# A feed-forward down product computed as seven half products over quadrants

## Chip, cores and metric

The kernel runs on one core of one Trainium2 chip. The metric is the device time of one execution in microseconds (us), as the median of several runs; lower is better. TensorE (PE in the profile) multiplies, VectorE (DVE) and ScalarE (ACT) work on elements, SyncE (SP) issues all the transfers.

## The reference, cut to what matters

Two batches of tokens (512 and 256, together T = 768) pass through two layers with the same weights. Each layer has a norm, two mixers, an output product with a residual, a second norm and a feed-forward block; a last norm ends the trunk.

```python
x = x + jnp.einsum('bsd,de->bse', merged, w_out)
h = rmsnorm(x, norm_ffn_g)
hid = jnp.square(jax.nn.relu(jnp.einsum('bsd,df->bsf', h, w_ff1)))     # 1024 -> 4096
return x + jnp.einsum('bsf,fd->bsd', hid, w_ff2)                       # 4096 -> 1024
```

## The kernel before, in words

Activations mostly lie with features in partitions, as tiles of 128 features by 768 tokens. Each fp32 operand of a dense product is split into a part rounded to fp32r ("hi") and the rest ("lo"), and a product is three passes: hi·hi, hi·lo and lo·hi. `wunit` (L148) loads 512 KB of weights in one transfer, rounds them on ScalarE (L156) and subtracts on VectorE (`sub`, L106, called in L157). `side[0]` is VectorE from the first layer's mixers on.

All dense products stand in one stream of items. An item's body runs matrix groups through `mm_group` (L215), and the next item's weights are made ahead by one item (`make_units`). `feat_dense` gives features in partitions and goes through the tokens in two ranges, `SPLITS`: 512 and 256. `tok_dense` gives tokens in partitions: six blocks of 128 tokens, 256 output columns wide. Accumulators of these groups come from the pool `pac`, three PSUM banks; five other banks are in the pool `pmx` (`pm`).

The program is recorded through a framework that schedules it: on each engine the instructions stand in the order that its scheduler chose, which is near the written one but interleaves neighbours, and each engine then goes through its own list in order.

The feed-forward block (L1047 to L1087) goes through the 4096 inner features in four chunks of 1024. Up: eight tiles of 128 features, each with 24 matmuls per token range; L1061 applies relu and the norm's factor on VectorE, L1062 squares on ScalarE, L1063 and L106 make hi and lo of the hidden tile. Down in the first layer: eight column tiles of `w_ff2`, each 24 matmuls per token range, and `evac2` adds the accumulator to the residual `xT` (L1070); in the last chunk it also feeds the next layer's norm (`Norm.add`: L288, L289, L297, L298) and stores `xT` (`spill`, L849). Down in the second layer: `tok_dense` in four slices of 256 columns, after `Last.to_tokens` has turned the residual around by 48 transposes (L796); `Last.add` adds (L802) and, in the last chunk, norms and stores each block of tokens as it is done.

```python
            nc.vector.tensor_tensor(x, x, acc[:, :n], op=ALU.add)                    # L1070, before
            out = Last(xT)                                                           # L1081
```

After the first layer's block the second layer begins with the values of its softmax mixer (`tok_dense`, L892, 256 or 288 columns wide): their evacuation (L877, L878) needs the tokens' 1/rms, which comes out of ones-matmuls over the norm's sums (L334), and small steps on ScalarE and VectorE (L337, L354 to L359).

## Time and profile before

| | |
|---|---|
| time, median of 3 runs | 3077.69 us (3076.8 to 3079.48) |
| profiled execution: span from first to last instruction | 3075.7 us |
| TensorE matmuls busy | 3051.5 us, 99% of the span |
| VectorE busy | 1574.4 us, 51% |
| ScalarE busy | 1229.8 us, 40% |
| granted TensorE clock, mean | 0.998 of full speed |

The page gives the span of the profiled execution; a time of its own is not listed beside the three runs, which lie 1.1 to 3.8 us above the span. "Busy" counts an engine's instructions with their overlap taken out. TensorE's busy share is near the whole, so what counts in most stages is how many matmul columns there are, and where another engine or a transfer makes TensorE wait.

### The profile page before, as it was taken

Reading aid. Unit: us, or ns where it says so; the run is one execution under the profiler, and the core shown is the slowest. Engines: PE = TensorE matmul, PEld = TensorE weight load, DVE = VectorE, ACT = ScalarE, POOL = GpSimd, SP = SyncE. Lnnn points to the kernel's source line nnn. Section 1 sums busy time; section 2 is a strip of 40 time slices with the busy share of each in tenths; the row PEclk is TensorE's granted clock in tenths of the full one; section 3 lists DMA queues with packets and bytes.
Section 4 is the critical chain, followed back from the end, with each engine's and each line's share of the span. In section 5 each row is a group of like instructions: output and inputs, shape, how many; then the busy total and the mean of one; then the engine's idle time right before and its main releaser. Section 6 shows DMA issues by size and latency. Waiting matters only on the chain.

```text
span 3075.7 us, 49458 instructions
## 1 busy us (share of the span) xinstructions
PE 3051.5 (99%) x20048; PEld 2763.5 (90%) x20048; DVE 1574.4 (51%) x3419; ACT 1229.8 (40%) x2709; POOL 7.5 (0%) x7
## 2 busy tenths in 40 slices
PE   8999999999999999999999999999999999999998
PEld 7988889999888888888899888899988889999998
DVE  5456667665445423333553666677744553333334
ACT  4555565544223313222343655655532233222133
POOL 0000000000000000000000000000000000000000
PEclk9999999999999999999999999999999999999999
DMA  6533322222422222222354233332233322222222
GB/s 210 186 80 84 90 77 82 67 73 72 134 93 78 62 68 63 62 62 65 98 166 137 73 84 89 83 94 69 59 112 98 103 62 62 62 62 62 63 69 69
DMA packets 371892, 268.05 MB, mean 87 GB/s; under 512 B 37552, under 2 KB 345040, under 8 KB 371664
## 3 DMA queue, kind: packets, MB, share of 16 engines
q1 hardware_dynamic: 371664, 264.89, 29.4%
q8 instruction: 158, 2.59, 0.4%
q14 instruction: 70, 0.57, 0.1%
HBM read 217.50 MB, written 47.33 MB: 86 GB/s over the span
## 4 chain that ended last, share of the span: by engine, by line
PE 95%; DMA 2%; DVE 2%; ACT 1%; SPq 0%; issue 0%; POOL 0%; ACTq 0%; DVEq 0%
PE acc L215 86%; PE op L524 2%; PE go L735 1%; PE pt L510 1%; PE sp L487 1%; PE up L713 1%; PE cp L657 1%; PE ap L695 1%; DMA l_dram<-b 0%; DMA v<-v_dram 0%; PE sp L483 0%; DMA raw<-in_w_in 0%; PE tp L764 0%; PE sp L481 0%; PE kp L684 0%
## 5 line engine op out<-in xcount | busy, mean ns | idle before, releaser
L215 PE MATMUL acc<-hh,whi 128*128 128x256 f32 (+1 forms) x2560 | 884.8, 346 | 0.3 <-DVE rl L1061 0.3
L215 PE MATMUL acc<-hl,whi 128*128 128x256 f32 (+1 forms) x2560 | 863.0, 337 | 0.0
L215 PE MATMUL acc<-hh,wlo 128*128 128x256 f32 (+1 forms) x2560 | 861.7, 337 | 0.0
L156 ACT CAST whi<-raw 128x1024 fp32r<-128x1024 f32 x320 | 335.7, 1049 | 602.7 <-PE acc L215 564.8
L215 PEld LDWEIGHTS acc<-hh,whi 128*128 128x128 f32 x2560 | 485.5, 190 | 55.5 <-DVE rl L1061 0.5
L215 PEld LDWEIGHTS acc<-hh,wlo 128*128 128x128 f32 x2560 | 484.8, 189 | 52.7
L215 PEld LDWEIGHTS acc<-hl,whi 128*128 128x128 f32 x2560 | 486.1, 190 | 41.6 <-issue 0.5
L106 DVE TENSOR_TENSOR wlo<-raw,whi 128x1024 fp32r<-128x1024 f32 (+1 forms) x317 | 388.3, 1225 | 155.0 <-ACT whi L156 152.4
L215 PE MATMUL acc<-whi,hh 128*128 128x256 f32 (+1 forms) x1344 | 390.1, 291 | 2.7 <-DVE vst L878 1.4
L215 PE MATMUL acc<-whi,hl 128*128 128x256 f32 (+1 forms) x1344 | 383.0, 285 | 3.0 <-DVE hl L289 2.8
L215 PE MATMUL acc<-wlo,hh 128*128 128x256 f32 (+1 forms) x1344 | 382.9, 285 | 0.8 <-POOL wlo L106 0.8
L215 PEld LDWEIGHTS acc<-whi,hl 128*128 128x128 f32 x1344 | 258.4, 192 | 5.1 <-DVE hl L289 3.6
L215 PEld LDWEIGHTS acc<-whi,hh 128*128 128x128 f32 x1344 | 258.3, 192 | 5.0 <-issue 2.6
L215 PEld LDWEIGHTS acc<-wlo,hh 128*128 128x128 f32 x1344 | 257.9, 192 | 1.1 <-POOL wlo L106 1.1
L215 PE MATMUL acc<-whi,hih 128*128 128x256 f32 x768 | 217.3, 283 | 0.0
L215 PE MATMUL acc<-whi,hil 128*128 128x256 f32 x768 | 217.3, 283 | 0.0
L215 PE MATMUL acc<-wlo,hih 128*128 128x256 f32 x768 | 217.3, 283 | 0.0
L1062 ACT ACTIVATE rl<-rl 128x512 f32<-128x512 f32 (+1 forms) x128 | 66.9, 523 | 274.5 <-DVE rl L1061 274.5
L215 PE MATMUL acc<-hil,whi 128*128 128x256 f32 (+1 forms) x512 | 172.4, 337 | 0.0
L215 PE MATMUL acc<-hih,whi 128*128 128x256 f32 (+1 forms) x512 | 172.3, 336 | 0.0
L215 PE MATMUL acc<-hih,wlo 128*128 128x256 f32 (+1 forms) x512 | 172.0, 336 | 0.0
L1061 DVE SCALAR_TENSOR_TENSOR rl<-acc,nr 128x512 f32<-128x512 f32 (+1 forms) x128 | 71.4, 558 | 181.9 <-PE acc L215 174.5
(232 smaller groups left out, 4785.3 us busy)
## 6 DMA issues: line engine op xcount, KB each, us to landing
raw<-in_w_in SPq DMA_DIRECT2D x152, 512.0 KB, 4.0
raw<-in_w_ff SPq DMA_DIRECT2D x128, 512.0 KB, 4.2
v_dram<-vst SPq DMA_DIRECT2D x72, 256.0 KB, 2.3
v<-v_dram SPq DMA_DIRECT2D x64, 128.0 KB, 4.7
raw<-in_w_branch_b SPq DMA_DIRECT2D x16, 512.0 KB, 4.3
raw<-in_w_out SPq DMA_DIRECT2D x16, 512.0 KB, 4.4
x_dram<-xT SPq DMA_DIRECT2D x16, 384.0 KB, 2.3
la_dram<-le SPq DMA_DIRECT2D x24, 256.0 KB, 3.4
```

The source lines that it names most:

```text
L106: eng.tensor_tensor(out, x, hi.bitcast(F32), op=ALU.subtract)
L156: nc.scalar.copy(hi, raw)
L215: nc.tensor.matmul(acc[:, :n], wt, xt, start=(k == 0 and j == 0), stop=(k == nkt - 1 and j == 2))
L487: nc.tensor.matmul(sp[hh][:, (g - 1) * 128:g * 128], q[g][pb, bs], k[g][pb, bs], start=True, stop=True)
L510: nc.tensor.transpose(pt[0:kx[g], g, hh, :], pr[hh][:, c0[g]:c0[g] + kx[g]], ident)
L524: nc.tensor.matmul(op[:, hh], v[ks, hh].rearrange("p s c -> p (s c)"), pT[g][ks, hh].rearrange("p s c -> p (s c)"), start=(g == 0), stop=( ...
L657: nc.tensor.matmul(cp[:, j, :], x[:, j, dc], cumT[:, d, :], start=(i == 0), stop=(i == 1))
L695: nc.tensor.matmul(ap[-1][:, j, :], ek[:, j, :], eq[:, j, :], start=True, stop=True)
L713: nc.tensor.matmul(up, x, y, start=(i == 0), stop=(i == 2))
L735: nc.tensor.matmul(op, x, y, start=(i == 0), stop=(i == len(mm) - 1))
L1061: nc.vector.scalar_tensor_tensor(r, acc[:, :n], 0.0, fnorm.r[:, t0:t0 + n], op0=ALU.max, op1=ALU.mult)
L1062: nc.scalar.activation(r, r, AF.Square)
```

## The change

The down product of the feed-forward block is written as Strassen's scheme in Winograd's form. The inner features come in eight chunks of 512; the tokens in two halves of 384 (`HALVES`), in the up product and the output product too. For each chunk, `quad_dense` has four items m = 0..3; item m computes the output feature tiles m and m + 4 for both halves of the tokens, from a 2 by 2 arrangement of weights (A11 to A22, each 256 by 128) and of hidden tiles (B11 to B22, each 256 by 384). Seven products take the place of eight. Each product is six matmuls of 384 columns (two inner tiles by three passes). Their operands are sums: S1 to S4 of weights (`wquad`, four VectorE operations, then hi and lo of each) and T1 to T4 of hidden tiles (`Quads.second`). The sums of products are made in PSUM: bank A takes A11·B11, S2·T2, S3·T3 and A22·T4 one after the other, and after each the running sum is added to one quadrant of `xT` on VectorE; bank C takes S1·T1 and S4·B22 in this way, bank B takes A12·B21. The banks come from `pmx`. The last two products of an item are kept in `later` and run between groups of what follows. In the last chunk the additions feed `Norm.add` (first layer) or the new `Last.add` (second layer).

Both layers now use this form, with features in partitions. In the second layer the result is turned around at the end: `Last.to_tokens` makes 12 transposes per m, those of the last m after all products, then the norm's factor, and 12 stores. The constants of the mixers (`dist`, `cumT`, `mask`, and the buffers `glT`, `wgate`) move from a pool that lasts into one that is opened at each layer's mixers, so they are loaded once more in the second layer.

```diff
+HT = T // 2
+HALVES = ((0, HT), (HT, HT))
...
+    def mixer_constants(pool):
+        dist = pool.tile([128, 3, 256], F32, name="dist")
+        cumT = pool.tile([128, 2, 256], F32R, name="cumT")
+        mask = pool.tile([128, 256], U8, name="mask")
         nc.sync.dma_start(out=dist, in_=a["alibi"])
...
+        scope.update(dist=dist, cumT=cumT, mask=mask,
+                     glT=pool.tile([98, T], F32R, name="glT"),
+                     wgate=pool.tile([98, 1024], F32R, name="wgate"))
...
+                if not stream and later:
+                    current.append(one_later())
...
+    later = deque()
+
+    def one_later():
+        if later:
+            yield from later.popleft()()
...
-                    for t0, n in SPLITS:
+                    for t0, n in splits:
                         yield from feat_tile(units[0], ci, x, t0, n, i + ci, evac)
+                        yield from one_later()
...
+    def split2(x, hi, lo):
+        nc.scalar.copy(hi, x)
+        sub(lo, x, hi)
+        return hi, lo
...
+        def first(self, p, x):
+            if self.b11 is None:
+                self.b11 = b3("b11h", F32R, (128, 2, HT)), b3("b11l", F32R, (128, 2, HT))
+            self.x[p] = x
+            self.ops["B11", p] = split2(x[:, 0:HT], *(y[:, p] for y in self.b11))
...
+        def second(self, p, y):
+            x = self.x[p]
+            b11, b12, b21, b22 = x[:, 0:HT], x[:, HT:T], y[:, 0:HT], y[:, HT:T]
+            t13, t24 = b3("t13"), b3("t24")
+            t1, t3, t2, t4 = t13[:, 0:HT], t13[:, HT:T], t24[:, 0:HT], t24[:, HT:T]
+            nc.vector.tensor_tensor(t1, b12, b11, op=ALU.subtract)
+            nc.vector.tensor_tensor(t3, b22, b12, op=ALU.subtract)
+            nc.vector.tensor_tensor(t2, b22, t1, op=ALU.subtract)
+            nc.vector.tensor_tensor(t4, b21, t2, op=ALU.subtract)
+            for z, names in ((y, ("B21", "B22")), (t13, ("T1", "T3")), (t24, ("T2", "T4"))):
+                hi, lo = split2(z, b3("qh", F32R), b3("ql", F32R))
+                for i, name in enumerate(names):
+                    self.ops[name, p] = hi[:, i * HT:(i + 1) * HT], lo[:, i * HT:(i + 1) * HT]
...
+    def wquad(w, m):
...
+        src = [w[:, (m + 4 * i) * 128:(m + 4 * i + 1) * 128].rearrange("(k p) c -> p k c", p=128) for i in range(2)]
+        nc.sync.dma_start(out=raw[:, 0:4], in_=src[0])
+        nc.sync.dma_start(out=raw[:, 4:6], in_=src[1][:, 2:4])
+        nc.sync.dma_start(out=raw[:, 6:8], in_=src[1][:, 0:2])
+        a11, a12, a22, a21 = (raw[:, 2 * i:2 * i + 2] for i in range(4))
+        s12, s43 = (b3(n, shape=(128, 4, 128)) for n in ("s12", "s43"))
+        s1, s2, s4, s3 = s12[:, 0:2], s12[:, 2:4], s43[:, 0:2], s43[:, 2:4]
+        ah, al = (wsp.tile([128, 6, 128], F32R, tag="w", name=n) for n in ("ah", "al"))
+        nc.vector.tensor_tensor(s1, a21, a22, op=ALU.add)
+        nc.vector.tensor_tensor(s2, s1, a11, op=ALU.subtract)
+        split2(raw[:, 0:6], ah, al)
+        nc.vector.tensor_tensor(s4, a12, s2, op=ALU.subtract)
+        nc.vector.tensor_tensor(s3, a11, a21, op=ALU.subtract)
+        ops = {n: (ah[:, 2 * i:2 * i + 2], al[:, 2 * i:2 * i + 2]) for i, n in enumerate(("A11", "A12", "A22"))}
+        for s, names in ((s12, ("S1", "S2")), (s43, ("S4", "S3"))):
+            hi, lo = split2(s, *(scope["ws"].tile([128, 4, 128], F32R, tag="ws", name=n) for n in ("sh", "sl")))
+            for i, n in enumerate(names):
+                ops[n] = hi[:, 2 * i:2 * i + 2], lo[:, 2 * i:2 * i + 2]
+        return ops
+
...
+                def product(an, bn, bank, dests):
+                    def g():
+                        if bank not in banks:
+                            banks[bank] = pm("w" + bank), True
+                        acc, new = banks[bank]
+                        banks[bank] = acc, False
+                        ah, al = units[0][an]
+                        for p in range(quads.n):
+                            bh, bl = quads.ops[bn, p]
+                            for j, (x, y) in enumerate(passes(ah[:, p], al[:, p], bh, bl)):
...
+                                nc.tensor.matmul(acc[:, :HT], x, y, start=(new and p == 0 and j == 0),
+                                                 stop=(p == quads.n - 1 and j == 2), skip_group_check=True)
+                        for i, k in dests:
+                            add_to(m + 4 * i, k, acc[:, :HT])
+                        yield quads.n * 3 * HT / 2400
+                    return g
+
+                yield from product("A11", "B11", "A", [(0, 0)])()
+                yield from one_later()
+                yield from product("S1", "T1", "C", [(1, 1)])()
+                yield from product("A12", "B21", "B", [(0, 0)])()
+                yield from one_later()
+                yield from product("S2", "T2", "A", [(0, 1)])()
+                yield from product("S4", "B22", "C", [(0, 1)])()
+                later.append(product("S3", "T3", "A", [(1, 1)]))
+                later.append(product("A22", "T4", "A", [(1, 0)]))
+            return f
+
+        for m in range(4):
+            add([lambda m=m: wquad(w, m)], body(m))
...
+            if t0 not in self.acc:
+                self.acc[t0] = b3("lacc", shape=(128, n))
+                nc.scalar.activation(self.acc[t0], x, AF.Square)
+            else:
+                sq = b3("lsq", shape=(128, n))
+                nc.scalar.activation(sq, x, AF.Square)
+                nc.vector.tensor_tensor(self.acc[t0], self.acc[t0], sq, op=ALU.add)
+            nc.scalar.activation(x, x, AF.Copy, scale=gfin[:, k:k + 1])
+            m = k % 4
+            self.left[m] -= 1
+            if self.left[m] == 0:
+                self.to_tokens(m)
...
+        def to_tokens(self, m):
+            last = len(self.y) == NT and not any(self.left)
+            if last:
+                r = self.rms()
+            for b in range(NT):
+                if b not in self.y:
+                    self.y[b] = b3("ya", shape=(128, 2, 384))
+                y = self.y[b]
+                tp = pm("tp", (128, 2, 128))
                 for i in range(2):
...
+                rb = r[:, b:b + 1]
+                z = b3("yb", shape=(128, 2, 128))
+                nc.scalar.activation(z, tp, AF.Copy, scale=rb)
+                nc.vector.tensor_scalar(y, y, rb, None, op0=ALU.mult)
+                out, row = (y_prompt, b) if b < 4 else (y_sample, b - 4)
+                out = out.rearrange("o s d -> (o s) d")[row * 128:(row + 1) * 128].rearrange("t (i c) -> t i c", i=2)
+                nc.sync.dma_start(out=out[:, :, 0:384], in_=y)
+                nc.sync.dma_start(out=out[:, :, 384:512], in_=z)
...
+        mixer_constants(mixers.enter_context(tc.tile_pool(name=f"mxc{l}", bufs=1)))
...
+        scope["ws"] = ffn.enter_context(tc.tile_pool(name=f"wsq{l}", bufs=7))
...
-        feat_dense(a["w_out"][l], 0, mg, evac, ncol=DM)
+        feat_dense(a["w_out"][l], 0, mg, evac, ncol=DM, splits=HALVES)
...
-        for c in range(4):
...
-                    nc.scalar.copy(hh, r)
-                    sub(hl, r, hh)
...
-            def evac2(k, t0, n, acc, xT=xT, c=c, norm=norm):
-                x = xT[k][:, t0:t0 + n]
-                nc.vector.tensor_tensor(x, x, acc[:, :n], op=ALU.add)
...
-            if not last:
-                feat_dense(w2, 0, hid, evac2, ncol=DM)
-                continue
-            if c == 0:
-                out = Last(xT)
-                weave([lambda b=b, i=i: out.to_tokens(b, i) for b in range(NT) for i in range(2)], 40)
-            for u in range(4):
-                tok_dense(lambda v, u=u, w2=w2: [(w2[v * 512:(v + 1) * 512, u * 256:(u + 1) * 256], 256)], 256, hid,
-                          lambda b, acc, u=u, c=c: out.add(b, acc, u, c))
...
+                r = f3("rl", shape=(128, n))
+                nc.vector.scalar_tensor_tensor(r, acc[:, :n], 0.0, fnorm.r[:, t0:t0 + n], op0=ALU.max, op1=ALU.mult)
+                nc.scalar.activation(q[0][:, t0:t0 + n], r, AF.Square)
+                if i < 2 and t0 == 0:
+                    chunks[c].first(i, q[0])
+                elif i >= 2 and t0:
+                    chunks[c].second(i - 2, q[0])
+
...
+            def add_to(k, half, acc):
+                t0 = half * HT
+                x = xT[k][:, t0:t0 + HT]
+                nc.vector.tensor_tensor(x, x, acc, op=ALU.add)
+                left[k, half] = left.get((k, half), 1 if k >= 4 and half == 0 else 2) - 1
+                if c < 7 or left[k, half]:
+                    return
+                if last:
+                    out.add(k, x, t0, HT)
+                    return
+                norm.add(k, x, t0, HT)
+                if left.get((k, 1 - half), 1) == 0:
+                    spill(k)
+
+            quad_dense(a["w_ff2"][l][c * 512:(c + 1) * 512, :], chunks[c], add_to)
+
+        for c in range(8):
+            tiles = [4 * c + i for i in (0, 2, 1, 3)]
+            for i, t in enumerate(tiles):
+                up(t)
+                if i == (3 if c == 7 else 0) and c:
+                    down(c - 1)
```

On TensorE, in the first layer's down product, the rows before are those of one accumulator that takes 24 matmuls in a row (`hih`, `hil` are hi and lo of a hidden tile, `whi`, `wlo` of the weights); the first of them are:

```order
L215 MATMUL acc_11745<-hih_11203,whi_11673 128x512
L215 MATMUL acc_11745<-hil_11204,whi_11673 128x512
L215 MATMUL acc_11745<-hih_11203,wlo_11674 128x512
L215 MATMUL acc_11745<-hih_11294,whi_11673 128x512
L215 MATMUL acc_11745<-hil_11295,whi_11673 128x512
```

Now, in a chunk of the first layer (wA_12193, wB_12209 and wC_12201 are the banks of item 0, wA_12253 is bank A of item 1; `qh`, `ql`, `b11h` are hi and lo of the hidden operands, `ah`, `sh`, `sl` of the weights):

```order
L341 MATMUL wB_12209<-qh_12076,al_12095 128x384
L341 MATMUL wA_12253<-b11h_11549,ah_12177 128x384
L341 MATMUL wA_12193<-qh_11931,sh_12102 128x384
L341 MATMUL wA_12193<-ql_11932,sh_12102 128x384
L341 MATMUL wA_12193<-qh_11931,sl_12103 128x384
L341 MATMUL wA_12193<-qh_12084,sh_12102 128x384
L341 MATMUL wA_12193<-ql_12085,sh_12102 128x384
L341 MATMUL wA_12193<-qh_12084,sl_12103 128x384
L341 MATMUL wC_12201<-qh_11923,sh_12106 128x384
L341 MATMUL wC_12201<-ql_11924,sh_12106 128x384
L341 MATMUL wC_12201<-qh_11923,sl_12107 128x384
```

A bank is taken up again after one or two products into other banks, and one matmul of the next item stands ahead of S2·T2.

On VectorE at the same places, before:

```order
L1070 TENSOR_TENSOR xT_10592<-xT_10592,acc_11745 128x512
L1070 TENSOR_TENSOR xT_10592<-xT_10592,acc_11771 128x256
L106 TENSOR_TENSOR wlo_11858<-raw_11855,whi_11857 128x1024
L1070 TENSOR_TENSOR xT_10594<-xT_10594,acc_11803 128x512
L1070 TENSOR_TENSOR xT_10594<-xT_10594,acc_11829 128x256
```

and now, in the middle of a chunk's four items (s12, s43 are sums of weights, sl and al their lo parts):

```order
L108 TENSOR_TENSOR sl_12246<-s12_12235,sh_12245 128x512
L1197 TENSOR_TENSOR xT_10603<-xT_10603,wA_12253 128x384
L1197 TENSOR_TENSOR xT_10609<-xT_10609,wA_12193 128x384
L1197 TENSOR_TENSOR xT_10611<-xT_10611,wC_12268 128x384
L1197 TENSOR_TENSOR xT_10603<-xT_10603,wB_12276 128x384
L314 TENSOR_TENSOR s12_12309<-raw4_12305 128x256
L318 TENSOR_TENSOR s43_12310<-raw4_12305 128x256
L1197 TENSOR_TENSOR xT_10609<-xT_10609,wA_12193 128x384
L108 TENSOR_TENSOR sl_12250<-s43_12236,sh_12249 128x512
L1197 TENSOR_TENSOR xT_10603<-xT_10603,wA_12253 128x384
L315 TENSOR_TENSOR s12_12309<-s12_12309,raw4_12305 128x256
L1197 TENSOR_TENSOR xT_10603<-xT_10603,wC_12268 128x384
```

Two additions to `xT` and one operation on weights per column tile have become seven additions and seven operations on weights per item.

On VectorE at the end of the first layer, before, from the last addition to `xT` to the first small steps of 1/rms (tv, tt):

```order
L1070 TENSOR_TENSOR xT_10606<-xT_10606,acc_15291 128x256
L106 TENSOR_TENSOR wlo_15350<-raw_15347,whi_15349 128x1024
L289 SCALAR_TENSOR_TENSOR hl_15285<-xT_10606,gmix_81,hh_15284 128x256
L298 TENSOR_TENSOR nacc_14829<-nacc_14829,sq_15319 128x256
L337 TENSOR_SCALAR tv_15386<-st_15381 128x4
L356 TENSOR_TENSOR tt_15388<-rt_15379 128x4
```

and now, from the next to last addition to `xT` on:

```order
L395 SCALAR_TENSOR_TENSOR hl_16001<-xT_10615,gmix_81,hh_16000 128x384
L404 TENSOR_TENSOR nacc_15712<-nacc_15712,sq_16004 128x384
L1197 TENSOR_TENSOR xT_10615<-xT_10615,wA_15915 128x384
L108 TENSOR_TENSOR wlo_16033<-raw_16029,whi_16032 128x1152
L395 SCALAR_TENSOR_TENSOR hl_16001<-xT_10615,gmix_81,hh_16000 128x384
L404 TENSOR_TENSOR nacc_15687<-nacc_15687,sq_16016 128x384
L108 TENSOR_TENSOR wlo_16063<-raw_16060,whi_16062 128x1024
L443 TENSOR_SCALAR tv_16098<-st_16094 128x3
L137 CAST cumT_16040<-mats0_16043 128x512
L138 CAST mask_16041<-mats1_16044 128x256
L462 TENSOR_TENSOR tt_16100<-rt_16092 128x3
```

Between `tv` and `tt` there now stand the casts of the reloaded constants, of which `cumT` lies in memory that the first layer's `xT` held.

## Rows read from the trace of the kernel before

**Rows 1.** Page, part 1: busy us (share of the span) and instructions of each engine.

```profile
PE 3051.5 (99%) x20048; PEld 2763.5 (90%) x20048; DVE 1574.4 (51%) x3419; ACT 1229.8 (40%) x2709; POOL 7.5 (0%) x7
```

**Rows 2.** Page, part 4: chain that ended last, shares of the span by engine.

```profile
PE 95%; DMA 2%; DVE 2%; ACT 1%; SPq 0%; issue 0%; POOL 0%; ACTq 0%; DVEq 0%
```

**Rows 3.** Busy time by stretch: both feed-forward blocks (length, engines, clock, DMA share, GB/s).

```profile
1009.00:1542.80 533.80, 533.46 (x3079) 472.19 (x3078) 204.20 (x297) 148.46 (x228) 0.00 (x0) 1.00 0.23 69
2518.00:3067.00 549.00, 548.06 (x3881) 516.34 (x3880) 202.35 (x359) 153.11 (x280) 0.00 (x0) 1.00 0.21 63
```

**Rows 4.** Groups of instructions by shape, down product: count, busy us, mean ns.

```profile
L215 PE MATMUL acc<-whi,hih 128*128 128x256 f32 x768 | 217.3, 283 | 0.0
...
L215 PE MATMUL acc<-hih,whi 128*128 128x512 f32 x256 | 100.0, 391 | 0.0
...
L215 PE MATMUL acc<-hih,whi 128*128 128x256 f32 x256 | 72.3, 282 | 0.0
```

**Rows 5.** TensorE in order of time, first layer's up product: start us, us.

```profile
1299.81 0.39 PE L215 MATMUL acc<-hh,wlo 128*128 128x512 f32 x1
...
1303.21 0.39 PE L215 MATMUL acc<-hh,wlo 128*128 128x512 f32 x1
1303.44 0.28 PE L215 MATMUL acc<-hh,whi 128*128 128x256 f32 x1
...
1305.95 0.28 PE L215 MATMUL acc<-hh,whi 128*128 128x256 f32 x1
```

**Rows 6.** TensorE in order of time, first values of the second layer, 288 columns.

```profile
1539.83 0.30 PE L215 MATMUL acc<-whi,hh 128*128 128x288 f32 x1
...
1540.63 0.29 PE L215 MATMUL acc<-whi,hh 128*128 128x288 f32 x1
```

**Rows 7.** VectorE groups by shape: weights' lo part, addition to `xT` from PSUM.

```profile
L106 DVE TENSOR_TENSOR wlo<-raw,whi 128x1024 fp32r<-128x1024 f32 x314 | 384.2, 1224 | 152.2 <-ACT whi L156 149.6 <-PE acc L215 0.5
...
L1070 DVE TENSOR_TENSOR xT<-xT,acc 128x512 f32<-128x512 f32 x32 | 22.0, 687 | 97.2 <-PE acc L215 97.2
```

**Rows 8.** VectorE in order of time, first layer's up product.

```profile
1303.64 0.69 DVE L1061 SCALAR_TENSOR_TENSOR rl<-acc,nr 128x512 f32<-128x512 f32 x1 [2.95 <-PE acc L215]
...
1307.47 1.23 DVE L106 TENSOR_TENSOR wlo<-raw,whi 128x1024 fp32r<-128x1024 f32 x1 [0.51 <-ACT whi L156]
1308.61 0.42 DVE L106 TENSOR_TENSOR hil<-rl,hih 128x256 fp32r<-128x256 f32 x1
```

**Rows 9.** VectorE in order of time, linear-attention stage, one right behind the other.

```profile
639.63 0.68 DVE L598 TENSOR_TENSOR gqk<-acc,nr 128x512 f32<-128x512 f32 x1
640.23 0.41 DVE L670 TENSOR_TENSOR eb<-eb,gqk 128x256 f32<-128x256 f32 x1
```

**Rows 10.** ScalarE groups by shape: rounding to fp32r.

```profile
L156 ACT CAST whi<-raw 128x1024 fp32r<-128x1024 f32 x316 | 331.0, 1047 | 600.3 <-PE acc L215 564.8 <-ACT sq L297 13.2 <-issue 12.2
...
L1063 ACT CAST hih<-rl 128x512 fp32r<-128x512 f32 x64 | 39.7, 620 | 2.0
```

**Rows 11.** In order of time, all engines, from the first layer's last sums to the second's first evacuation.

```profile
1538.63 0.75 DVE L289 SCALAR_TENSOR_TENSOR hl<-xT,gmix,hh 128x512 fp32r<-128x512 f32 x1 [0.79 <-ACT hh L288]
...
1543.02 0.95 PE L334 MATMUL st<-eye,nacc 128*128 128x1 f32 x8
...
1547.64 0.47 DVE L878 SCALAR_TENSOR_TENSOR vst<-acc,rt,vst 128x256 fp32r<-128x256 f32 x1
```

**Rows 12.** In order of time, all engines, the end of the program.

```profile
3065.78 0.28 PE L215 MATMUL acc<-wlo,hih 128*128 128x256 f32 x1
...
3067.30 0.41 DVE L802 TENSOR_TENSOR xt<-xt,acc 128x256 f32<-128x256 f32 x1
...
3068.38 4.47 SPq L828 DMA_DIRECT2D y_sample<-xt  x8
```

**Rows 13.** Transfers by issuing line: KB each, median us to landing.

```profile
raw<-in_w_ff SPq DMA_DIRECT2D x128, 512.0 KB, 4.2
...
x_dram<-xT SPq DMA_DIRECT2D x16, 384.0 KB, 2.3
```

129 lines of the change are left out of this document (53 added, 76 removed).

## The prediction

> **What bounds the kernel now.** I read the page from the top. TensorE's matmuls are busy for 99% of the span [rows 1], and TensorE has 95% of the chain that ended last [rows 2], so time is won or lost there first. By stretch, both feed-forward blocks have no gap on TensorE to speak of: 533.5 of 533.8 us and 548.1 of 549.0 us busy, at a granted clock of 1.00 [rows 3]. VectorE has 204 and 202 us in them, ScalarE 148 and 153 us: work that is hidden. So the price of a matmul is its distance to the next one, not its duration, since matmuls overlap. In order of time, 16 matmuls of 512 columns take 1303.44 - 1299.81 = 3.63 us, 0.2269 us each, and 21 of 256 take 2.51 us, 0.1195 us each [rows 5]. No row has 384 columns. The straight line between the two gives 0.1732 us, and a third width lies on that line: six matmuls of 288 columns take 0.80 us, 0.1333 us each, where the line says 0.133 [rows 6]. The bounds for 384 are thus 0.1195 and 0.2269, and I take 0.1732.
>
> **TensorE's sum.** The down product before: one of three passes shows 256 matmuls of 512 and 256 of 256 columns in the first layer, 768 of 256 in the second [rows 4]; times three, 768 x 0.2269 + 768 x 0.1195 = 266.0 us and 2304 x 0.1195 = 275.3 us. Now each layer has 8 chunks x 4 items x 7 products x 6 matmuls = 1344 of 384 columns, 232.8 us. That is 33.2 us less in the first layer and 42.5 us less in the second, where the narrow matmuls go as well: **75.7 us**. The up product keeps its columns: 24 x (0.2269 + 0.1195) = 8.31 us per tile before, 48 x 0.1732 = 8.31 us now. Work that TensorE does beside this (the transposes) keeps its count.
>
> **What VectorE gets.** Its price too is a distance: a subtraction of 1024 columns lasts 1.23 us, but the next starts 1.14 us after it [rows 8]; one of 512 with a PSUM operand lasts 0.68 us and is followed after 0.60 us [rows 9]. The line through these gives 0.33 us for 256 columns, 0.465 for 384, 0.87 for 768. In the repeating part, per chunk: 28 additions to `xT` (13.0 us); for four items 16 weight sums, 8 lo parts of 512 and 4 of 768 (13.6 us); 4 lo parts of the up weights (4.6 us); 8 relu steps, 8 sums T, 2 and 6 lo parts of hidden tiles (13.6 us). Together 44.8 us, and TensorE needs 28 x 1.039 + 4 x 8.31 = 62.4 us. ScalarE's roundings, 1.05 us for 1024 and 0.62 us for 512 columns [rows 10], come to some 23 us per chunk and are hidden. So on the whole VectorE has room: 72% where it had 38%.
>
> Not everywhere: in the four items that run one after the other (26 products, 27.0 us of TensorE; the other two lie in the next up tiles) the order shows 26 additions, 12 weight sums, 6 lo parts of 512, 2 of 768 and 2 of 1024: 12.1 + 4.0 + 3.6 + 1.7 + 2.3 = **23.7 us, 88%**. What is late there matters, since a PSUM bank can be written again only when its addition has been read: the last matmul ends 0.16 us after the next could start, VectorE begins 0.04 us later [rows 5, 8], and the addition lasts 0.55 us (0.687 at 512 columns [rows 7], by the line); with as much back to TensorE again, **0.79 us**. The order puts 13 matmuls (2.25 us) between A11·B11 and S2·T2 and 12 (2.1 us) between S2·T2 and S3·T3, so an addition may come 1.3 us late, that is behind one 768 or two small operations. Laying the listed pieces of a group end to end at these prices, every addition is in time, by 0.1 to 1.5 us; twice per group VectorE itself stands idle some 0.9 us, because an addition that waits for A22·T4 is ahead of work that could go. Such margins do not all hold. Lower bound: no wait. Upper bound: full durations (27.8 us, from 1.224 and 0.687 us [rows 7]) plus the two idle waits, 29.7 - 27.0 = 2.7 us per group. I take 0.5 us, near the lower one, since VectorE's distances and not its durations are what rows 8 and 9 show: 14 groups, **+7 us** (0 to 38). At the first group of a chunk the work on hidden tiles is just behind VectorE; there I look for the waits first.
>
> The Trainium skill speaks against this reading: "VectorE: DVE Perf Modes", section "The DRAIN you can't avoid", has the next operation start only when the pipe is empty. By that an operation would cost its whole duration, which is the upper bound above. The distances of rows 8 and 9 are 0.09 and 0.08 us shorter than the durations, so here the trace differs.
>
> **Ends of the blocks.** In the first layer's last chunk each finished quadrant feeds `Norm.add` as well. VectorE then has, over the last 28 products (29.1 us): 28 additions 13.0, 16 `hl` at 0.53 (0.75 us at 512 columns [rows 11], 0.07 over a plain one) 8.5, 14 norm sums 6.5, two sets of weight work 7.3, two lo parts of the next layer's first weights 2.6: 37.9 us. The excess is 8.8 us; 2.3 us of it comes after the last addition, and some 2 us of older work is carried in. **+8 us** (4 to 12). In the second layer `Last.add` has only the sums on VectorE and nine copies of transposes: 13.0 + 6.5 + 3.0 + 7.3 = 29.8 us, about even with TensorE, **+3 us** (0 to 8).
>
> Between the layers `cumT` is cast on VectorE ahead of the 1/rms steps, and waits for the last spill of `xT`, whose memory it gets. From the norm's ones-matmuls to the first evacuation it took 4.6 us [rows 11], hidden by three blocks of values in three banks (72 matmuls of 288 columns, 9.6 us). The spill lands 2.3 us after its issue when alone, and a 512 KB load in front of it takes 4.2 us [rows 13]. So the cast comes 3 to 8 us after the last addition, the evacuation 4 to 5 us later: **+2 us** (0 to 5). The other reloads and the gate weights' loads, which are now behind it on SP, have the next slices' weights behind them, each needed some 17 us later.
>
> The tail was 3075.7 - 3066.06 = 9.6 us after the last matmul [rows 12], with stores of five blocks already out. Now nothing is out: last addition, square, sum (about 0.55 us each), the ones-matmuls and small steps (2.4 to 4.6 us, the latter by rows 11), then 12 stores of 3.1 MB through SP; eight stores took 4.47 us of it [rows 12], so 12 take up to 6.7 us, and a landing 2.3 us. 11 to 15 us; I take 12.6, **+3 us** (1 to 6).
>
> **Sum.** 3075.7 - 75.7 + 7 + 8 + 3 + 2 + 3 = 3023 us of span. The runs lie 2.0 us above the profiled span in the median, so **3025 us**.
>
> **Rivals.** (1) VectorE sets the pace in the groups of four items: each loses the upper bound, 14 x 2.7 = 38 us in place of 7, 3056 us. For it: 88% is an average over an in-order engine with waits on two others. Against: the distances measured. The rule on DRAIN that the Trainium skill gives (above) would lead to this case.
>
> (2) Slower than before: every re-use of a bank pays the round trip. Its place is banks A and C, four re-uses per item, 64 items: 256 x 0.79 = 202 us on top of 3025 - 7, so 3220 us. It decides from 0.23 us per re-use on ((75.7 - 16) / 256). For it: the dependence is real in every item. Against: the order has 2 us of other products in between. The Trainium skill's "PSUM — Partial Sum Buffer", section "PSUM bank collisions raise a hardware error", asks to guard a bank as a whole; that adds no waiting where a bank has one reader, as here, and no row of before shows an accumulation that goes on after a read.
>
> (3) The change doesn't do what it says: 384 columns cost as 512. Then 2688 + 3072 matmuls lose 0.0537 us each, 309 us; rows 6 make that very unlikely.
>
> (4) Cheaper: no wait inside the groups and half of the end terms, 3010 us.
>
> **Numbers.** Forecast 65% (its own range 3014 to 3040), rival 1 18%, rival 4 11%, rival 2 5%, rival 3 1%. The range reaches to 3006 and 3056: forecast, most of rival 4 and half of rival 1. A difference of 0.2% (6 us) is about what runs of this kernel can tell. Rival 1 reaches into "same" only at its far end: faster 92%, same 2%, slower 6%.
>
> **What would show it.** Matmuls into banks A, B, C 0.173 us apart, and both blocks near 500 us plus ends (right), or gaps before S2·T2, S3·T3 or S4·B22 whose releaser is the addition at L1197 (rivals 1 and 2). VectorE 70 to 75% busy within the blocks. A stretch of some 40 us before the first layer's end in which TensorE waits for L1197, L395 or L404. A wait of the second layer's first evacuations for the cast of `cumT`. A tail of 11 to 15 us. The prediction is wrong if VectorE's additions last longer against TensorE's writes than 0.55 us, or if scheduled interleaving leaves additions behind longer work than the order lets me see.

## The result and the profile after

The changed kernel takes 3029.18 us (median of 4 runs, 3026.97 to 3029.88), the kernel before took 3077.24 us beside it: a ratio of 0.984 (95% interval 0.983 to 0.986), 48.1 us less. The forecast was 3025 us, the range 3006 to 3056. The profiled execution has a span of 3028.1 us (forecast 3023). In runs 8 and 10 one execution each lay far above the others (7471 and 5900 us); their times are medians of the rest.

The page first, its parts 1, 4 and 5 (one line of each):

```profile
PE 2990.7 (99%) x18908; PEld 2797.1 (92%) x18908; DVE 1947.8 (64%) x4177; ACT 1318.0 (44%) x2790; POOL 7.5 (0%) x7
...
PE 95%; DVE 3%; DMA 1%; ACT 1%; issue 0%; SPq 0%; POOL 0%; DVEq 0%; ACTq 0%
...
L1197 DVE TENSOR_TENSOR xT<-xT,wA 128x384 f32<-128x384 f32 x256 | 136.1, 548 | 20.3 <-PE wA L341 18.8
```

Against [rows 1, 2], TensorE is busy 61 us less and is still the bound; VectorE went from 51 to 64%. The addition out of a bank lasts 0.548 us (the forecast had 0.55).

Where did the 47.6 us of span (3075.7 - 3028.1) come from? A mark that both kernels have is the last rounding of the merged values, ahead of each layer's output product. The groups by tile end with the first and last start. Before, first and second layer:

```profile
L1024 ACT CAST mgh<-sgb x16: 407/514/620, 877.9 to 938.6; 128x512 fp32r<-128x512 f32 x8, 128x256 fp32r<-128x256 f32 x8
...
L1024 ACT CAST mgh<-sgb x16: 407/514/620, 2389.5 to 2450.2; 128x512 fp32r<-128x512 f32 x8, 128x256 fp32r<-128x256 f32 x8
```

And after:

```profile
L1144 ACT CAST mgh<-sgb x16: 406/514/620, 876.2 to 936.9; 128x512 fp32r<-128x512 f32 x8, 128x256 fp32r<-128x256 f32 x8
...
L1144 ACT CAST mgh<-sgb x16: 406/514/620, 2368.7 to 2429.4; 128x512 fp32r<-128x512 f32 x8, 128x256 fp32r<-128x256 f32 x8
```

1.7 us was gained ahead of the first mark, 19.1 us between the marks (1511.6 to 1492.5: first feed-forward block, boundary, second mixers) and 26.8 us from the second mark to the end (625.5 to 598.7). By the forecast's terms these should have been 19.7 (33.2 - 3.5 - 8 - 2) and 33 (42.5 - 3.5 - 3 - 3). The first layer came out as forecast, the second 6 us short.

Stretches next (length, busy time of PE, PEld, DVE, ACT and POOL, granted clock, DMA share, GB/s): a group of four items, a whole chunk, then parts of the first layer's last two chunks, then the tail.

```profile
1045.31:1072.73 27.42, 27.42 (x157) 26.95 (x157) 24.76 (x50) 8.53 (x13) 0.00 (x0) 1.00 0.34 97
1072.89:1135.68 62.79, 62.79 (x362) 62.30 (x361) 46.56 (x85) 21.80 (x32) 0.00 (x0) 1.00 0.24 68
1447.30:1459.10 11.80, 9.37 (x44) 8.91 (x43) 11.65 (x23) 5.38 (x8) 0.00 (x0) 0.86 0.15 44
1452.00:1455.00 3.00, 0.62 (x4) 0.30 (x2) 3.00 (x7) 0.53 (x1) 0.00 (x0) 1.00 0.00 0
1455.00:1458.00 3.00, 2.95 (x11) 2.98 (x12) 3.00 (x7) 0.72 (x2) 0.00 (x0) 0.61 0.44 132
...
1489.00:1518.78 29.78, 25.12 (x128) 21.98 (x127) 29.52 (x61) 17.78 (x33) 0.00 (x0) 0.97 0.37 129
1515.00:1518.00 3.00, 1.41 (x6) 1.13 (x5) 3.00 (x5) 1.61 (x4) 0.00 (x0) 0.85 0.36 142
...
3012.00:3015.00 3.00, 3.00 (x17) 3.00 (x17) 0.48 (x3) 0.41 (x2) 0.00 (x0) 0.52 0.00 0
3018.00:3021.00 3.00, 0.00 (x0) 0.00 (x0) 0.72 (x2) 0.00 (x0) 0.00 (x0) 0.50 0.99 353
```

A chunk in the repeating part takes 62.8 us where the columns alone were put at 62.4, and VectorE is busy for 46.6 of them, 74%. In a group of four items VectorE is busy for 24.8 of 27.4 us, 90% (forecast 88% of 27.0). At the first layer's end time is lost in two places. At 0.1733 us each (run 2 below) the 44 matmuls of 1447.30 to 1459.10 need 7.6 of its 11.8 us, and the 128 of 1489.00 to 1518.78 need 22.2 of its 29.8, with VectorE busy for 29.5; between the two (1459.1 to 1489.0) nothing is lost. The largest hole of this block is in 1452 to 1455. In order of time TensorE has there:

```profile
1452.29 0.34 PE L341 MATMUL wA<-b11h,al 128*128 128x384 f32 x1
1455.05 0.41 PE L341 MATMUL wC<-qh,sh 128*128 128x384 f32 x1 [2.43 <-DVE xT L1197]
...
1455.95 0.52 PE L341 MATMUL wC<-ql,sh 128*128 128x384 f32 x1
1456.27 0.52 PE L341 MATMUL wC<-qh,sl 128*128 128x384 f32 x1
```

and VectorE:

```profile
1449.82 0.55 DVE L1197 TENSOR_TENSOR xT<-xT,wA 128x384 f32<-128x384 f32 x1
1450.28 0.55 DVE L297 TENSOR_TENSOR t<-hq,t 128x384 f32<-128x384 f32 x1
1450.75 0.95 DVE L108 TENSOR_TENSOR ql<-hq,qh 128x768 fp32r<-128x768 f32 x1
1451.62 1.82 DVE L108 TENSOR_TENSOR ql<-t,qh 128x768 fp32r<-128x768 f32 x2
1453.36 0.41 DVE L314 TENSOR_TENSOR s<-raw 128x256 f32<-128x256 f32 x1
...
1454.36 0.55 DVE L1197 TENSOR_TENSOR xT<-xT,wC 128x384 f32<-128x384 f32 x1
```

The addition of S1·T1 out of bank C starts 4.5 us after the addition ahead of it, behind the rest of the work on the last chunk's second hidden pair (3.1 us) and three weight sums (1.0 us), and S4·B22 into bank C cannot start. The seven other chunk ends don't show this, since there an up tile lies between the hidden work and the products. Behind the hole the matmuls are 0.32 us apart instead of 0.173, at a granted clock of 0.61 over that stretch; the ten to 1458.83 lose 1.5 us. The rows also show VectorE's distances: 0.46 us behind an addition of 384 columns, 0.87 behind a lo part of 768.

The end of the program, in order of time:

```profile
3007.48 0.34 PE L341 MATMUL wA<-qh,sl 128*128 128x384 f32 x1
3007.90 0.55 DVE L1197 TENSOR_TENSOR xT<-xT,wA 128x384 f32<-128x384 f32 x1
...
3008.50 0.45 PE L341 MATMUL wA<-qh,ah 128*128 128x384 f32 x1 [0.68 <-DVE xT L1197]
...
3009.50 0.34 PE L341 MATMUL wA<-qh,al 128*128 128x384 f32 x1
...
3011.64 2.29 PE L938 MATMUL st<-eye,lacc 128*128 128x1 f32 x12 [1.80 <-DVE lacc L903]
...
3015.52 2.30 ACT L927 ACTIVATE yb<-tp,fr 128x256 f32<-128x256 f32 x6 [0.90 <-DVE fr L465]
3016.02 0.61 SPq L932 DMA_DIRECT2D y_prompt<-yb  x1
...
3024.30 0.58 SPq L932 DMA_DIRECT2D y_sample<-yb  x1
```

The last matmul ends at 3009.84; 18.3 us follow where 9.6 followed before [rows 12]. The small steps take 6.2 us, at half clock on TensorE; the twelve stores are issued over 8.9 us, and the last lands 3.2 us later. The first three rows show the round trip of a bank with no other product in between: 1.02 us between two matmuls that are else 0.17 apart, so 0.85 us lost (0.79 in the forecast).

### The profile page after: what moved, and what is told of

Read it like the earlier page. It is cut to its first block, busy times and chain, and to the rows that moved or that the text cites. A ratio compares the mean times of both kernels' runs of the same rounds, so it can differ in the third digit from the quotient of the medians.

```text
span 3028.1 us, 48402 instructions
## 1 busy us (share of the span) xinstructions
PE 2990.7 (99%) x18908; PEld 2797.1 (92%) x18908; DVE 1947.8 (64%) x4177; ACT 1318.0 (44%) x2790; POOL 7.5 (0%) x7
## 3 DMA queue, kind: packets, MB, share of 16 engines
q1 hardware_dynamic: 391088, 265.16, 29.5%
## 4 chain that ended last, share of the span: by engine, by line
PE 95%; DVE 3%; DMA 1%; ACT 1%; issue 0%; SPq 0%; POOL 0%; DVEq 0%; ACTq 0%
PE acc L223 71%; PE wA L341 8%; PE wC L341 4%; PE op L630 2%; PE wB L341 2%; PE pt L616 1%; PE go L841 1%; PE sp L593 1%; PE up L819 1%; PE cp L763 1%; PE ap L801 1%; DVE xT L1197 1%; PE sp L589 0%; PE sp L587 0%; PE tp L870 0%; DVE hl L395 0%
## 5 line engine op out<-in xcount | busy, mean ns | idle before, releaser
L223 PE MATMUL acc<-hh,whi 128*128 128x384 f32 (+2 forms) x2560 | 881.2, 344 | 0.0
L223 PE MATMUL acc<-hl,whi 128*128 128x384 f32 (+2 forms) x2560 | 860.0, 336 | 0.0
L223 PE MATMUL acc<-hh,wlo 128*128 128x384 f32 (+2 forms) x2560 | 859.4, 336 | 0.0
L108 DVE TENSOR_TENSOR wlo<-raw,whi 128x1024 fp32r<-128x1024 f32 (+1 forms) x253 | 309.9, 1226 | 88.4 <-ACT whi L162 85.8
L1197 DVE TENSOR_TENSOR xT<-xT,wA 128x384 f32<-128x384 f32 x256 | 136.1, 548 | 20.3 <-PE wA L341 18.8
L270 ACT CAST sh<-s 128x512 fp32r<-128x512 f32 x128 | 78.1, 619 | 142.5 <-DVE s L315 77.2
L108 DVE TENSOR_TENSOR ptx<-pt,ptx 128x256 fp32r<-128x256 f32 (+1 forms) x192 | 80.8, 421 | 89.4 <-ACT ptx L620 86.8
L223 PE MATMUL acc<-spl,whi 128*128 128x256 f32 (+1 forms) x384 | 129.4, 337 | 0.0
L223 PE MATMUL acc<-sph,whi 128*128 128x256 f32 (+1 forms) x384 | 129.3, 337 | 0.0
L223 PE MATMUL acc<-sph,wlo 128*128 128x256 f32 (+1 forms) x384 | 129.0, 336 | 0.0
```

Of the source, the lines that this page charges most:

```text
L108: eng.tensor_tensor(out, x, hi.bitcast(F32), op=ALU.subtract)
L223: nc.tensor.matmul(acc[:, :n], wt, xt, start=(k == 0 and j == 0), stop=(k == nkt - 1 and j == 2))
L270: nc.scalar.copy(hi, x)
L1197: nc.vector.tensor_tensor(x, x, acc, op=ALU.add)
```

## Experiments

**1. Eight plain half products.** `wquad` splits A11, A12, A22 and A21 only, hidden tiles are split without sums, and an item runs

```diff
-yield from product("A11", "B11", "A", [(0, 0)])()      # ... seven in all
+for i in range(2):
+    for k in range(2):
+        acc = pm("w")
+        yield from product("A%d1" % (i + 1), "B1%d" % (k + 1), acc, True, (i, k))
+        yield from product("A%d2" % (i + 1), "B2%d" % (k + 1), acc, False, (i, k))
```

> Halves of 384 tokens, chunks of 512 and items of four quadrants stay; each item takes eight plain half products, each quadrant two of them in one bank with one addition, and no sums S and T. Theory (the gain is the missing eighth product, less the waits that its sums bring): 64 items x 1.039 us = 66.5 us more TensorE than the changed kernel, and the waits for VectorE go away, which I add up to 10 to 23 us in its trace: 3072 to 3086 us, about where the kernel before stands. Rival (the gain comes from the new widths and chunks, 384 columns in place of 512 and 256): 3029 us or less.

3071.81 us, ratio 0.998 (0.997 to 0.999), just below the range expected. So the rest of the change by itself, the halves and chunks above all, is worth about 5 us, and the rest of the gain is the missing product: of its 66.5 us, 42.6 are left (3071.8 - 3029.2), and some 24 us go to what the sums bring. The rival falls.

**2. No sums.**

```diff
-nc.vector.tensor_tensor(t1, b12, b11, op=ALU.subtract)  # and T2 to T4, S1 to S4, their hi and lo
+for name, other in (("T1", "B21"), ("T2", "B22"), ("T3", "B21"), ("T4", "B22")):
+    self.ops[name, p] = self.ops[other, p]
```

> The seven products per item and their additions stay, but the sums S1 to S4 and T1 to T4 and their roundings and lo parts are left out (the products take A11, A12, A22 and B21, B22 in their place, so the output is not the reference's). VectorE has 28.6 us per chunk in place of 44.8. Theory (TensorE waits only where VectorE has more to do than TensorE, at the ends of the two blocks): 12 us less in the first layer, 5 in the second, 2 to 5 in the repeating part, 3009 us (3005 to 3014). Rival (waits are the round trip of a bank through its addition, whatever else VectorE does): 3023 to 3030 us.

3008.57 us, 20.6 less than the changed kernel, as expected. Where it is gained is read from two marks per layer: first and last relu step (`rl`), and last matmul into bank A. The changed kernel, first and second layer:

```profile
L1182 DVE SCALAR_TENSOR_TENSOR rl<-acc,nr x64: 547/557/558, 1011.3 to 1447.3; 128x384 f32<-128x384 f32 x64
L341 PE MATMUL wA<-qh,al x64: 334/334/522, 1056.9 to 1518.5; 128*128 128x384 f32 x64
...
L1182 DVE SCALAR_TENSOR_TENSOR rl<-acc,nr x64: 545/557/558, 2503.8 to 2940.5; 128x384 f32<-128x384 f32 x64
L341 PE MATMUL wA<-qh,al x64: 334/334/346, 2549.3 to 3009.5; 128*128 128x384 f32 x64
```

Without the sums:

```profile
L1170 DVE SCALAR_TENSOR_TENSOR rl<-acc,nr x64: 556/558/559, 1010.4 to 1444.0; 128x384 f32<-128x384 f32 x64
L329 PE MATMUL wA<-qh,al x192: 333/334/343, 1047.9 to 1504.2; 128*128 128x384 f32 x192
...
L1170 DVE SCALAR_TENSOR_TENSOR rl<-acc,nr x64: 556/558/559, 2490.4 to 2924.0; 128x384 f32<-128x384 f32 x64
L329 PE MATMUL wA<-qh,al x192: 333/334/347, 2527.9 to 2988.2; 128*128 128x384 f32 x192
```

First to last relu step: 436.0 and 436.7 us with sums, 433.6 and 433.6 without, so 5.5 us. Between these marks lie six groups of four items per layer, 12 in all (168 additions to `xT`); the groups of the last two chunks stand behind the last relu step. From the last relu step to the last product: 71.2 and 69.0 us against 60.2 and 64.2, so 11.0 us at the first layer's end and 4.8 at the second's. The repeating part hardly waits; the ends do. Without the sums it does not wait at all, and shows the plain distance of 384 columns, 433.60 / 2502 = 0.1733 us:

```profile
1010.40:1444.00 433.60, 433.60 (x2502) 433.33 (x2501) 209.92 (x323) 104.15 (x152) 0.00 (x0) 1.00 0.23 67
```

In its ends this kernel still waits for additions, 1.1 and 0.6 us.

**3. No interleaving by hand.**

```diff
-later.append(product("S3", "T3", "A", [(1, 1)]))
-later.append(product("A22", "T4", "A", [(1, 0)]))
+yield from product("S3", "T3", "A", [(1, 1)])()
+yield from product("A22", "T4", "A", [(1, 0)])()
```

> S3.T3 and A22.T4 of an item follow S4.B22 at once instead of being put between products of the next item or up tile. Theory (a bank is free again 0.79 us after its last matmul, and the order hides this): A22.T4 follows S3.T3 in the same bank with nothing between, 64 x 0.79 = 51 us more, some of it more where an addition stands behind other work on VectorE: 3080 us (3070 to 3095). Rival (an addition's read doesn't hold up the next accumulation): 3029 us.

3044.72 us: 15.5 more, not 51. The test did not produce what it meant to: in the trace the scheduler has put 9 other matmuls (1306.26 to 1307.81 us) between S3·T3 and A22·T4 of its own accord. First to last relu step costs 437.5 us, 1.5 more than with `later`; 8.5 us are lost in the second layer's end (77.5 against 69.0), where transposes now stand right behind additions and TensorE waits 3.3 us in all for what they need, seven times. Another 3.8 us go between the layers, where TensorE waits 1.9 us for the lo part of the next weights. So 64 bare round trips were not tried, and neither theory nor rival is settled; the one round trip seen bare is the 0.85 us of the row above.

**4. More work for VectorE.**

```diff
 nc.vector.tensor_tensor(x, x, acc, op=ALU.add)
+if c < 7 and more:                 # more: the product is A11.B11, S2.T2 or A22.T4
+    nc.vector.tensor_tensor(b3("more", shape=(128, HT)), x, x, op=ALU.add)
```

> Three further additions of 384 columns on VectorE per item, in chunks 0 to 6 of both layers, behind the additions of A11.B11, S2.T2 and A22.T4; nobody reads their result. Theory (VectorE's price is the distance, 0.465 us): the four items that run one after the other take 23.7 + 12 x 0.465 = 29.3 us of VectorE beside 27.0 us of TensorE, 2.3 us late in each of 14 groups, of which 0.4 us is there already: 3056 us (3045 to 3080). Rival (its price is the whole duration, 27.8 + 12 x 0.55 = 34.4 us): 7.4 us in each group, 3127 us or more. No change at all would say that VectorE has far more room than either.

3053.93 us, 24.7 more: the price by distances holds, the one by durations (3127) falls. First to last relu step takes 444.3 us in the first layer and 444.6 in the second, 8.1 more on average, 1.35 us for each of six groups; the two ends, with one such group each, take 6.6 us more. Over all 14 groups that is 1.6 us each, where 1.9 was worked out. So a VectorE operation that follows at once costs its distance here, 0.46 us, and not its duration, 0.55. The Trainium skill, "VectorE: DVE Perf Modes", section "The DRAIN you can't avoid", has the next operation wait for the empty pipe, but adds that one that is not held starts earlier. The prediction left out the second half; the distances here agree with it.

**5. The hidden work spread.** After this the ends were the question.

```diff
+steps = [lambda: sums(0), lambda: sums(1), lambda: parts(y, ("B21", "B22")),
+         lambda: parts(t13, ("T1", "T3")), lambda: parts(t24, ("T2", "T4"))]
+if self.spread and p == 1:         # last chunk only; product() runs one behind its additions
+    chores.extend(steps)
```

> The last chunk's work on its second hidden pair (four sums T, three roundings with their lo parts), which stands in one piece ahead of the additions of the products before it, is cut into five pieces, one behind each of the next products. Theory (from there to the end of the block VectorE has more to do than TensorE, so what is saved at one place is waited for at another): the 2.4 us wait at the first product's second bank goes, the waits after it grow by as much, 3029 us (3026 to 3031). Rival (it is a wait of that place, with the granted clock that falls behind it): 4 us less in the first layer and 2.4 in the second, 3023 us.

3024.81 us, ratio 0.983 (0.981 to 0.984), 4.4 less; the intervals of the two ratios overlap, the runs (3023.91 to 3025.03) do not. My theory falls: the stretch to the last product is 66.7 us in place of 71.2 in the first layer and 66.8 in place of 69.0 in the second, so what was saved at that place was not waited for again. The stretches give back 6.7 us, the rival's 6.4; of the spans' difference (5.1) 1.2 us are lost again between the layers and 0.4 in the tail. An in-order queue in which one addition stands behind some 4 us of other work loses TensorE's time at once, though VectorE is busy all the while.

**6. Squares for the norm on GpSimd.**

```diff
+side[0] = nc.gpsimd
 norm.add(k, x, t0, HT)
+side[0] = nc.vector
```

> In the last chunk of the first layer the 14 additions of squares for the next norm go to GpSimd, nothing else. Theory (VectorE sets the end of the first layer): 14 x 0.465 = 6.5 us less there, 3023 us (3021 to 3026); nothing in the second layer. Rival (the waits are chains of single dependences, or GpSimd's accesses slow VectorE down): 3029 us or more.

3033.01 us, 3.8 more than the changed kernel. The work left VectorE, but the `hl` steps beside it became longer. In the changed kernel and in this one (ns: shortest, median, longest):

```profile
L395 DVE SCALAR_TENSOR_TENSOR hl<-xT,gmix,hh x16: 608/612/617, 1486.7 to 1521.7; 128x384 fp32r<-128x384 f32 x16
```

```profile
L395 DVE SCALAR_TENSOR_TENSOR hl<-xT,gmix,hh x16: 607/899/1366, 1486.0 to 1523.8; 128x384 fp32r<-128x384 f32 x16
```

GpSimd's addition lasts 1276 ns there. VectorE's additions out of a bank kept their 0.54 us. The 16 `hl` take 14.3 us instead of 9.8, so most of the 6.5 us hoped for is gone: the first layer's end is 70.7 us against 71.2. The Trainium skill, "SBUF — State Buffer", section "SBUF: two separate sides", says that a VectorE operation with two operands in SBUF and a GpSimd operation that reads SBUF take one shared port pair in turns, as an exclusive lock; the rows agree: `hl` reads two tiles in SBUF, an addition out of a bank reads one. The rival holds as far as the missing gain goes. The time on top is not shown to come from GpSimd: of the 1.7 us between the two profiled spans, 1.6 lie in the second layer's end (70.6 against 69.0), where the code is the same. There a gap of 2.4 us is followed by another granted clock; in the changed kernel and in this one:

```profile
2949.00:2952.00 3.00, 3.00 (x19) 3.00 (x19) 3.00 (x9) 0.30 (x2) 0.00 (x0) 1.00 0.61 180
```

```profile
2949.00:2952.00 3.00, 3.00 (x13) 3.00 (x13) 3.00 (x8) 0.62 (x1) 0.00 (x0) 0.66 0.54 159
```

**7. Weight sums of the last two chunks on GpSimd as well.**

```diff
-nc.vector.tensor_tensor(s1, a21, a22, op=ALU.add)      # and S2, S4, S3
+eng.tensor_tensor(s1, a21, a22, op=ALU.add)            # eng: nc.gpsimd for c >= 6
```

> As the run before, and the 16 weight sums S of each of the last two chunks of both layers on GpSimd. Theory: VectorE is relieved of 6.5 + 2 x 5.3 us at the end of the first layer and 2 x 5.3 us at the end of the second, more than it is late there (some 12 and 5 us): 3013 us (3010 to 3018), with no gap over 1 us on TensorE in the last two chunks. Rival (GpSimd is too slow for the chain S1, S2, S4, or takes VectorE's accesses): no better than the run before, with waits of VectorE's lo parts for GpSimd.

3034.30 us: no better. Over the first layer's end the `hl` take 0.94 us in the mean (0.61 in the changed kernel) and the `sl` parts 0.86 (0.69); GpSimd's sums take 0.93 to 1.09 us each where VectorE's take 0.42. The ends are 72.5 and 72.3 us against 71.2 and 69.0. The rival holds, mostly by the longer operations: the `sl` parts wait for the roundings of the sums 6.6 us over the whole run, instead of 4.4.

**8. Without the large stores.** The line `nc.sync.dma_start(out=out[:, :, 0:384], in_=y)` is taken out.

> The six stores of three quarters of the output are left out at the end; the six stores of the last quarter stay. Theory (the end is the drain of 3.1 MB that can start only when all is known): the stores take 4 us instead of 9, and the tail from the last product is 13 us instead of 18, 3024 us (3022 to 3026). Rival (the end is the chain of small steps and the landing of the last store): 3028 to 3029 us.

3024.63 us, ratio 0.983 (0.981 to 0.985). In its trace 12.4 us follow the start of the last matmul, with them 18.6: 2.36 MB cost 6.2 us of the tail, and the theory holds. (The products end 1.9 us later in that execution, so less shows in the time.) The remaining 12 us are small steps and the rest of the stores. The run takes out six issues together with their bytes and does not separate the two; that the transfer engines are 99% busy in the changed kernel speaks for the bytes.

**9. The last chunk by eight plain products.**

```diff
-chunks = [Quads(2) for _ in range(8)]
+chunks = [Quads(2, c == 7) for c in range(8)]          # plain: eight products, no S, no T
```

> Only the last chunk of each layer takes eight plain half products per item, the other seven chunks stay with seven. From the last relu step to the last product the changed kernel takes 71.2 us in the first layer and 69.0 in the second, and without the sums (run e2_no_sums) 60.2 and 64.2. Theory (the ends lose what the sums of the last chunk put ahead of additions on VectorE): 4.2 us of TensorE more in each layer, but 16 additions in place of 28, no sums of weights or of hidden tiles: 64 to 66 us in the first layer, 66 to 68 in the second, 3020 us (3016 to 3024). Rival (the waits at the ends come from the norm's own work, hl and the sums of squares): the 8.3 us show in full, 3033 to 3038 us.

3018.31 us, ratio 0.981 (0.980 to 0.982), 10.9 less than the changed kernel, with 8.3 us more of matmuls. From the last relu step to the last product: 62.4 us in the first layer (1446.9 to 1509.3) against 71.2, 68.4 in the second against 69.0 (66 to 68 were expected), and TensorE has no wait at all at the first layer's end:

```profile
1446.90:1509.30 62.40, 62.40 (x360) 62.03 (x359) 53.61 (x99) 27.50 (x46) 0.00 (x0) 1.00 0.35 110
```

The norm's own work, which is still there, was not the cause by itself. The run takes out 12 additions of the last chunk along with its sums; run 2, which keeps the additions, gets nearly as far (1.1 us of waits). The first evacuation of the second layer follows the last product after 6.7 us (1509.3 to 1516.0) instead of 10.4.

**10. The final norm by halves**, on top of run 9.

```diff
-self.left[m] -= 1
-if self.left[m] == 0:
-    self.to_tokens(m)
+h = t0 // HT
+self.left[m, h] -= 1
+if self.left[m, h] == 0:
+    self.to_tokens(m, h)                               # rms, scaling and stores of this half
```

> As the run before, and the second layer's final norm and its stores by halves of 384 tokens: the first half's 1/rms, scaling and six stores follow its own last addition, four half products (4.2 us) before the end. Theory (the tail is a chain of some 6 us of small steps and then the drain of what is left to store, 12 us for all): only half is left to drain behind the last chain, the tail from the last product is 13 to 15 us in place of 18.6, 4 us less than the run before. Rival (the small steps of the second half queue behind the first half's work on ScalarE, VectorE and SP, and the drain is bound by when it may start at all): within 1 us of the run before.

3018.87 us. The time is the rival's, the reason is not. The tail did shrink, from 17.1 to 12.4 us, but the products before it end 4.3 us later, counted from the last relu step (72.7 against 68.4). The waits of TensorE and a stretch of its end show why:

```profile
PE st L972 <- DVE lacc L937: 3.6, 2, 1.8
```

```profile
2997.00:3000.00 3.00, 2.13 (x12) 2.13 (x13) 1.00 (x4) 1.25 (x4) 0.00 (x0) 0.71 0.00 0
```

The ones-matmuls of the first half wait 1.8 us for its sum of squares ahead of products that could go, and the clock granted behind that wait is 0.71.

**11. The same, ones-matmuls later.**

```diff
+if h and self.held is not None:                        # first half's rms: after the next quadrant
+    held, self.held = self.held, None
+    self.to_tokens(*held)
```

> As the run before, and the first half's ones-matmuls and transposes come two half products (12 matmuls, 2.08 us) later in TensorE's order. Theory (the run before shortened the tail from 17.1 to 12.4 us, and lost as much because these matmuls, which wait 1.8 us for the sum of squares, stood ahead of the last two quadrants in TensorE's order, with the granted clock falling behind the wait): no such wait, the last quadrants end some 4 us earlier and the tail stays below 13 us: 3014 us (3012 to 3016). Rival (what the halves gain in the tail is lost again in stores that overlap scaling, wherever the small steps stand): 3018 to 3019 us.

3015.83 us, ratio 0.980 (0.979 to 0.982): the best version here, 13.4 us below the changed kernel. The tail is 13.3 us and the stretch before it 68.9. Against run 9 the spans differ by 3.3 us, but the intervals of the ratios overlap, so this last step is shown by the trace more than by the times.

## Why the prediction was right, point by point

| term of the sum, us | forecast | measured | from |
|---|---|---|---|
| TensorE's columns | -75.7 | about that | 0.1733 us per matmul, run 2 |
| waits in the groups | +7 (14 groups) | +5.5 (12 groups) | changed kernel and run 2 |
| end of the first layer | +8 | +11.0 | same, with one group |
| end of the second layer | +3 | +4.8 | same, with one group |
| boundary | +2 | +0.8 | below |
| tail | +3 | +8.7 | 18.3 against 9.6 |
| span | 3023 | 3028.1 | |

The line between 256 and 512 columns held: matmuls of 384 columns are 0.173 us apart. VectorE at 88% within a group, priced by distances, held too (90%); run 4 tells that price from the one by durations, and run 2 shows rival 1 (2.7 us per group) at a sixth of its price, 0.46 us (5.5 us in 12 groups). The forecast had 0.5. Rival 2 (0.79 us at each re-use) has the right round trip, 0.85 us, but the order hides it in the repeating part. Rival 3 falls with the distance (its price left out the output product's 768 matmuls, 41 us more). Rival 4 has nearly no waits in the groups, and falls by the end terms.

The **tail** is the term that was mis-sized most: +8.7 us, beyond its bound of 6. The step from eight stores in 4.47 us to "12 take up to 6.7 us" counted stores and not bytes: the eight hold 128 KB each, 1.0 MB, the twelve 3.1 MB. Those moved at 353 GB/s with the transfer engines 99% busy, their issues took 8.9 us, and the landing 3.2 instead of 2.3. Run 8, with 2.36 MB less, is 6.2 us shorter there.

The **end of the first layer** was expected to wait because VectorE has 37.9 us of work beside 29.1 over the last 28 products. (Two sets of weight work are 6.8 us by the prediction's own prices, not 7.3; 37.4 would have been right, and 29.3 in the second layer.) That place and mechanism held: the last 29.8 us lose 7.6, with VectorE busy throughout. What the sum lacked is the hole at 1452, well ahead of those products, where the last chunk's hidden work and three weight sums stand ahead of an addition: 4.2 us with the clock behind it. The "some 2 us of older work" that the forecast carried in was not there: nothing is lost between the two places, and VectorE itself waits 0.69 us for TensorE at 1485. Run 5 agrees: it gains 4.5 us in the first layer and 2.2 in the second. The place was named ("the work on hidden tiles is just behind VectorE") but for the first group of each chunk; it shows only where no up tile lies between. Run 9 takes out all waits of this end by taking out the sums, and 12 of the 28 additions, of one chunk in eight.

The **boundary** came out near its size for another reason. The cast of `cumT` comes 5.8 us after the last addition to `xT` (1520.00), as forecast (3 to 8), and the first evacuation 3.0 us after it (1528.85, forecast 4 to 5), but TensorE did not wait:

```profile
1525.51 0.16 DVE L443 TENSOR_SCALAR tv<-st 128x3 f32<-128x3 f32 x1 [0.26 <-PE st L440]
1525.81 0.43 DVE L137 CAST cumT<-mats 128x512 fp32r<-128x512 f32 x1
```

The three blocks of values covered the evacuation. (The 4.6 us read from [rows 11] for the kernel before end at the evacuation on VectorE; the one on ScalarE, L877, began at 1546.90, after 3.9 us.) The loss there is the first matmuls of 288 columns, seven of which ran 0.24 us apart, 0.107 more than in [rows 6], behind the waits of the last products: 0.8 us.

With the measured terms 3075.7 - 75.7 + 5.5 + 11.0 + 4.8 + 0.8 + 8.7 = 3030.8. The 1.7 us gained ahead of the first block make it 3029.1; 1.0 us is left over and not explained. Since run 2 still waits 1.1 and 0.6 us in its own ends, these cost rather 12.1 and 5.4 us, and then 2.7 us are not explained.

That the sum came within some 5 us is in part luck. Its mechanism held, but the ends and the tail were 10.5 us too cheap together, which 4.4 us in the other direction (groups, boundary, and the 1.7 us that no term had) and the unexplained part took back.

## What to carry to other kernels

A saving on the bound engine is kept in the steady part if the other engines' distances, not their durations, fit beside it; then look at the ends, where nothing lies between an engine's backlog and the instruction that needs it. There it can pay to leave the scheme: one chunk in eight with more matmuls and fewer sums was faster. And a reduction over everything ahead of the output puts all of its stores behind the last product: count the bytes that can no longer leave early, and split the reduction so that half of them can.

## What the runs showed of the hardware

A gap of 2.4 us on TensorE was followed by a granted clock of 0.61 over the next 3 us in the first layer of the changed kernel (the lower level, 1.2 GHz, for part of it), while the same gap in the second layer was followed by a clock of 1.00; in run 6 that second gap was followed by 0.66. So a gap of one length can cost 1.5 us more or nothing, also at a place where the code of two kernels is the same. Whether it differs from one execution of a kernel to the next is not shown, with one profile of each.

GpSimd does not relieve VectorE for nothing: beside its additions of two tiles in SBUF, VectorE's operations on two tiles in SBUF took up to 1.37 us instead of 0.61, those out of a bank stayed at 0.54.
